# Attention probabilities go through an SBUF-to-SBUF transfer and are transposed as fp32r, with four lane steps from scores to transposes

## The chip, the cores and the metric

The kernel runs on one core of a Trainium2 chip. The metric is the device time of one execution in microseconds (us); less is better. TensorE is called PE below, VectorE DVE, ScalarE ACT, GpSimd POOL, and SyncE SP. SP issues nearly all transfers here, in one queue.

## What is computed

One layer of a bidirectional hybrid encoder is applied to two groups of tokens with the same weights: 1024 sample tokens (eight tiles of 128) and 256 prompt tokens (two tiles), width 2048. The input is normalised and projected, three groups of heads work on the projection, and their outputs are joined and projected back:

```
proj = rms_norm(x, norm_g) @ w_in
o_ssd = two chunked state-space scans (one per direction), gated and normalised
o_att = window attention of 8 heads: |t-s| <= 128, ALiBi, a sink logit per head
o_mem = attention of 4 heads to 256 memory rows:
    sm = einsum('bthd,bmhd->bhtm', mq, mk) * d ** -0.5
    pm = softmax(sm)
    o_mem = einsum('bhtm,bmhd->bthd', pm, mv) * silu(z_mem)
y = x + concat[o_ssd, o_att, o_mem] @ w_out
```

All data are fp32. The change lies in o_att and o_mem, between the softmax and the product with the values.

## The kernel before

**The main work** is the projections. Tokens are handled in two groups of five tiles. A weight block is walked in 16 steps of k (128 rows of the weights each). For every step, 256 KB of weights are loaded into a tile wraw (four buffers) and split by wsplit (L200) into a rounded high part wh (ACT, L202) and a rest wl (DVE, L203), three buffers each. Three products, high by high, low by high and high by low, then run as fp32r matmuls (L254 to L256 in block_tok, L289 to L291 in block_feat). In block_tok a step of k is 15 matmuls of 512 columns. In block_feat it is 12 of 320 columns.

**The side work** (attention, scan, preparation) is written as Python generators, put into two lanes by queue (L135). After each step of k, pump (L155) adds the block's rate (RATES, L32) to what each lane is owed and runs as many generator steps; a step ends at a yield. In block_feat the rates are halved. So a rate of 1.55 on lane 0 means that 1.55 yields of lane 0 pass in a step of k, and the number of yields between two parts of a generator sets how much main work is written between them. A scheduler then lists the instructions for every engine: an engine takes, in the order written, what its own model of times calls ready. The chip runs each engine's list strictly in order, and so does SP with its transfers: a transfer whose data are not there holds up all transfers behind it.

**Window attention**, attn(t) (L583), is on lane 0. For each of the ten token tiles it makes four rounds rr, each with one query head of either of two key groups kv. scores(rr) (L627) makes the scores on PE (psc, L635 and L636), adds the distance on DVE (L637), takes the exponential on ACT (L641) and scales by the sum on DVE (L645). The result stays in lg, two halves of 128 x 385 fp32 (256 of its columns are used for tiles at a sequence's end, 384 elsewhere). turn_(rr) (L649) transposes it on PE in blocks of 128 x 128 into ppt (L657) and copies that to pT on ACT (L658). values(half) (L662) multiplies with the values for two rounds.

**Memory attention**, mem_attn(t) (L697), is also on lane 0 and has two rounds of two heads: scores(hp) (L724) ends with L744 in a tile mpr of 128 x 512, turn_(hp) (L748) transposes it in four blocks into pmt (L752), and values(hp) (L761) follows.

The transposes of probabilities take fp32 data and an fp32 identity, ident. That is the fp32r tile identr under another type. Other transposes (pq L617, pk L501, pmq L713, pxs L843) take fp32r data and identr.

Working tiles of lane 0 share the tag wa, with five buffers (WA, L29): q, squares, split queries, gates and outputs. lg and mpr share the tag lg with two buffers.

Of the kernel before, what the change touches and what calls it, by code (L numbers as in the profile page):

```python
# [10 lines left out]
F32 = mybir.dt.float32  # L11
F32R = mybir.dt.float32r
# [7 lines left out]
P = 128  # L20
# [8 lines left out]
CH, WB, RB, WA, WBB = 4, 3, 4, 5, 4  # L29
RBB = 3  # L30

RATES = ({'kv': (2.0, 1.0), 'mq': (2.4, 1.6), 'z0': (2.2, 1.7), 'z1': (2.2, 1.7)},  # L32
         {'kv': (1.2, 1.5), 'x': (1.75, 1.85), 'q': (1.6, 2.5), 'za': (1.6, 2.5), 'z0': (1.55, 2.6),
          'z1': (1.55, 2.65), 'mq': (1.55, 2.8), 'zm': (1.55, 2.85), 'o': (1.95, 1.9)})
FAR = 1e30

UNITS = (0, 4, 1, 5, 2, 6, 7, 3, 8, 9)
# [6 lines left out]
def hymba_encoder_kernel(  # L44
# [7 lines left out]
    V, A, G, T, S = nc.vector, nc.scalar, nc.gpsimd, nc.tensor, nc.sync  # L52
# [33 lines left out]
    identr = const([P, P], "identr", F32R)  # L86
    ident = identr.bitcast(F32)
# [495 lines left out]
    def attn(t):  # L583
        lo, hi = (0, NS) if t < NS else (NS, NT)
        k0, k1 = max(lo, t - 1), min(hi, t + 2)
        na = k1 - k0
        nk = na * P
        d0 = (k0 - (t - 1)) * P
        s0 = k0 if t < 4 else k0 - 3
        grp, ti = divmod(t, 5)  # L590
        tc_ = slice(ti * P, (ti + 1) * P)
        q = w2("q")
        S.dma_start(q, q_d[t])
        yield
        sq = w2("sq")
        A.activation(sq, q, AF.Square)
        ss = sm.tile([P, 8], F32, tag="s8", name="qss", bufs=4)
        V.reduce_sum(out=ss, in_=hv(sq), axis=AX.X)
        r = sm.tile([P, 8], F32, tag="s8", name="qr", bufs=4)
        rsqrt(r, ss, 1.0 / 64, 8)  # L600
        G.tensor_tensor(out=r, in0=r, in1=steep, op=ALU.mult)
        for _ in range(3):
            yield
        q3 = hv(q)
        V.tensor_mul(q3, q3, hb(r, 8, 64))
        yield
        qT = []
        for b in range(2):
            qh = mp.tile([P, 4, 2, 64], F32R, tag="wa", name="qh", bufs=WA)
            qb = q3[:, 4 * b:4 * b + 4, :]  # L610
            A.activation(qh[:, :, 0, :], qb, AF.Copy)
            V.tensor_sub(qh[:, :, 1, :], qb, qh[:, :, 0, :].bitcast(F32))
            yield
            ps = psum("pq")
            qf = qh.rearrange("p a b d -> p (a b d)")
            for a in range(4):
                T.transpose(ps[:, a * P:(a + 1) * P].bitcast(F32R), qf[:, a * P:(a + 1) * P], identr)  # L617
            o = mp.tile([P, 512], F32R, tag="qT", name="qT", bufs=2)
            A.activation(o, ps, AF.Copy)
            qT.append(o)  # L620
        z = w2("za")
        S.dma_start(hv(z, 4), zT_d[0][grp][:, :, tc_])
        yield
        ns8 = nsink.rearrange("p (v r) -> p r v", v=2)
        state_ = {}

        def scores(rr):  # L627
            lg = mp.tile([P, 2, 385], F32, tag="lg", name="lg", bufs=2)
            G.tensor_copy(lg[:, :, nk:nk + 1], ns8[:, rr, :].unsqueeze(2))  # L629
            nm = sm.tile([P, 2], F32, tag="m2", name="nm", bufs=10)  # L630
            for kv in range(2):
                h = 4 * kv + rr
                ps = psum("psc")
                st = qT[kv][:, rr * P:(rr + 1) * P]
                T.matmul(ps[:, :nk], st, kT[:, kv, s0 * P:s0 * P + nk], start=True, stop=False)  # L635
                T.matmul(ps[:, :nk], st, kL[:, kv, s0 * P:s0 * P + nk], start=False, stop=True)  # L636
                V.tensor_tensor_reduce(out=lg[:, kv, :nk], in0=pdist[:, d0:d0 + nk], in1=ps[:, :nk], scale=2.0 ** -(h + 1),  # L637
                                       scalar=nsink[:, h:h + 1], op0=ALU.add, op1=ALU.min, accum_out=nm[:, kv:kv + 1])
            den = sm.tile([P, 2], F32, tag="m2", name="den", bufs=10)
            for kv in range(2):  # L640
                A.activation(lg[:, kv, :nk + 1], lg[:, kv, :nk + 1], AF.Exp, scale=-1.0, bias=nm[:, kv:kv + 1],  # L641
                             accum_out=den[:, kv:kv + 1])
            V.reciprocal(out=den, in_=den)
            for kv in range(2):
                V.tensor_scalar(out=lg[:, kv, :nk], in0=lg[:, kv, :nk], scalar1=den[:, kv:kv + 1], scalar2=0.5,  # L645
                                op0=ALU.mult, op1=ALU.mult)
            state_[rr] = lg

        def turn_(rr):  # L649
            lg = state_.pop(rr)  # L650
            if rr % 2 == 0:
                state_["pT"] = mp.tile([P, 2, 2, 384], F32, tag="pT", name="pT", bufs=1)
            pT = state_["pT"]
            for kv in range(2):
                pt = psum("ppt")
                for a in range(na):
                    T.transpose(pt[:, a * P:(a + 1) * P], lg[:, kv, a * P:(a + 1) * P], ident)  # L657
                A.activation(pT[:, kv, rr % 2, :nk], pt[:, :nk], AF.Copy)  # L658

        oT = w2("oT")  # L660

        def values(half):  # L662
            pT = state_.pop("pT")
            po = psum("po")
            for a in range(na):
                for kv in range(2):
                    T.matmul(hv(po[kv * 64:kv * 64 + 64, :2 * P], 2), v_all[:, s0 + a, kv * 64:kv * 64 + 64],  # L667
                             pT[:, kv, :, a * P:(a + 1) * P], start=(a == 0), stop=(a == na - 1))
            c = slice(half * 2 * P, (half + 1) * 2 * P)
            V.tensor_mul(oT[:, c], po[:, :2 * P], z[:, c])  # L670

        scores(0)
        yield
        scores(1)
        yield
        yield
        turn_(0)
        yield
        scores(2)
        yield  # L680
        turn_(1)
        yield
        scores(3)
        yield
        values(0)
        yield
        turn_(2)
        yield
        turn_(3)
        yield  # L690
        yield
        values(1)
        yield
        S.dma_start(oT_d[0][grp][:, :, tc_], hv(oT, 4))


    def mem_attn(t):  # L697
# [3 lines left out]
        q = qr.bitcast(F32)  # L701
# [20 lines left out]
        st_ = {}  # L722

        def scores(hp):  # L724
            ps = psum("pms")
            for j in range(2):
                h = 2 * hp + j
                c = slice(h * P, (h + 1) * P)
                o = ps[:, j * 256:(j + 1) * 256]
                T.matmul(o, qh[:, c], mkH[:, h, :], start=True, stop=False)  # L730
                T.matmul(o, qh[:, c], mkL[:, h, :], start=False, stop=False)
                T.matmul(o, ql[:, c], mkH[:, h, :], start=False, stop=True)
            m = sm.tile([P, 2], F32, tag="m2", name="mm", bufs=10)
            V.reduce_max(out=m, in_=hv(ps, 2), axis=AX.X)
            V.scalar_tensor_tensor(out=m, in0=m, scalar=-1.0, in1=r[:, 2 * hp:2 * hp + 2], op0=ALU.mult, op1=ALU.mult)
            pr = mp.tile([P, 512], F32, tag="lg", name="mpr", bufs=2)
            den = sm.tile([P, 2], F32, tag="m2", name="mden", bufs=10)
            for j in range(2):
                A.activation(pr[:, j * 256:(j + 1) * 256], ps[:, j * 256:(j + 1) * 256], AF.Exp,
                             scale=r[:, 2 * hp + j:2 * hp + j + 1], bias=m[:, j:j + 1], accum_out=den[:, j:j + 1])  # L740
            V.reciprocal(out=den, in_=den)
            for j in range(2):
                c = slice(j * 256, (j + 1) * 256)
                V.tensor_scalar(out=pr[:, c], in0=pr[:, c], scalar1=den[:, j:j + 1], scalar2=0.5,  # L744
                                op0=ALU.mult, op1=ALU.mult)
            st_[hp] = pr

        def turn_(hp):  # L748
            pr = st_[hp]
            pt = psum("pmt")  # L750
            for a in range(4):
                T.transpose(pt[:, a * P:(a + 1) * P], pr[:, a * P:(a + 1) * P], ident)  # L752
            if hp == 0:
                st_["pT"] = mp.tile([P, 2, 768], F32, tag="pT", name="mpT", bufs=1)
            pT = st_["pT"][:, hp, :512]
            A.activation(pT, pt, AF.Copy)
            st_[hp] = pT
# [13 lines left out]

        scores(0)
        yield
        scores(1)
        yield
        yield
        turn_(0)
        yield
        turn_(1)
        yield  # L780
        values(0)
        yield
        values(1)
        S.dma_start(oT_d[1][grp][:, :, tc_], hv(oT, 4))
# [713 lines left out]
    mp = beside.enter_context(tc.tile_pool(name="mp", bufs=2))  # L1498
# [178 lines left out]
```

## Time and profile before

| what | value |
|---|---|
| time, median of 3 runs | 1805.68 us (1805.18 to 1806.63) |
| the profiled execution's own time | 1804.94 us |
| its span, first to last instruction | 1803.2 us |
| PE busy | 1791.4 us (99%) |
| DVE, ACT, POOL busy | 1210.3, 902.3, 456.6 us |
| bytes moved | 290.58 MB, 161 GB/s on average |

In the profile, a group of instructions is told by line, engine, operation and the names of the tiles it writes and reads (out<-in). A busy time is the union of the instructions' durations. For matmuls those durations are modelled and overlap, so what one matmul costs the queue is read from the starts of neighbours or from the chain, not from its own duration. "Idle before" is the time in which the engine did nothing ahead of such an instruction, with what ended that. SPq is SP's own instruction stream.

### The profile page before, as it was taken

What the parts mean: (1) busy time and instruction counts of PE and PEld (TensorE: products, weight loads), DVE (VectorE), ACT (ScalarE), POOL (GpSimd) and SP (SyncE); (2) the same over time, 40 slices, a digit from 0 to 9 for tenths busy, and PEclk for the clock granted to TensorE, in tenths of its full rate; (3) what the DMA queues carried; (4) which work ended last, traced back from release to release, by engine and by line L of the source; (5) the groups of instructions that cost most, each with busy time, mean ns of one, the idle gap of its engine ahead of it and who ended that gap; (6) DMA issues with size and microseconds to landing.
All of it is one profiled execution on the core that took longest, in us unless ns stands there. A gap on an engine that the chain in (4) does not pass through costs nothing.

```text
span 1803.2 us, 30420 instructions
## 1 busy us (share of the span) xinstructions
PE 1791.4 (99%) x10546; PEld 1607.0 (89%) x10546; DVE 1210.3 (67%) x2303; ACT 902.3 (50%) x1999; POOL 456.6 (25%) x772
## 2 busy tenths in 40 slices
PE   9999999999999999999999999999999999999999
PEld 8789999999887799999989988887898888899999
DVE  5595788877657877675755766556775653867665
ACT  6554455444445756464435645544474533543332
POOL 0105888861110000000000001101100000058775
PEclk9999999999999999999999999999999999999999
DMA  8654454446544544344336355457785554644442
GB/s 299 190 178 122 137 151 152 126 134 217 168 134 152 177 133 139 121 132 133 118 95 192 113 164 173 128 181 233 230 269 162 180 189 142 215 154 147 141 144 79
DMA packets 198891, 290.58 MB, mean 161 GB/s; under 512 B 18960, under 2 KB 80464, under 8 KB 198736
## 3 DMA queue, kind: packets, MB, share of 16 engines
q1 hardware_dynamic: 198592, 288.57, 51.4%
q8 instruction: 83, 1.36, 0.3%
q14 instruction: 72, 0.59, 0.1%
q10 hardware_dynamic: 144, 0.06, 0.0%
HBM read 231.12 MB, written 57.44 MB: 160 GB/s over the span
## 4 chain that ended last, share of the span: by engine, by line
PE 87%; issue 5%; DMA 3%; DVE 2%; ACT 1%; POOL 1%; SPq 0%; ACTq 0%; DVEq 0%; POOLq 0%
PE acc L254 13%; PE acc L256 13%; PE acc L255 12%; PE acc L1194 6%; PE acc L1192 6%; PE acc L1193 6%; PE acc L289 5%; PE acc L290 4%; PE acc L291 4%; PE accm L1193 2%; PE accm L1192 2%; PE accm L1194 2%; PE py L924 2%; PE po L667 1%; PE ppt L657 1%
## 5 line engine op out<-in xcount | busy, mean ns | idle before, releaser
L203 DVE TENSOR_TENSOR wl<-wraw,wh 128x512 fp32r<-128x512 f32 (+1 forms) x480 | 340.5, 711 | 273.8 <-ACT wh L202 265.0
L254 PE MATMUL acc<-wh,xH 128*128 128x512 f32 (+1 forms) x1248 | 482.7, 387 | 0.2 <-ACT wh L202 0.2
L255 PE MATMUL acc<-wl,xH 128*128 128x512 f32 (+1 forms) x1248 | 472.2, 378 | 0.6 <-DVE wl L203 0.4
L256 PE MATMUL acc<-wh,xL 128*128 128x512 f32 (+1 forms) x1248 | 472.4, 379 | 0.0
L202 ACT ACTIVATE wh<-wraw 128x512 fp32r<-128x512 f32 (+1 forms) x480 | 293.4, 615 | 348.4 <-PE acc L256 189.5
L255 PEld LDWEIGHTS acc<-wl,xH 128*128 128x128 f32 x1248 | 234.9, 188 | 43.7 <-DVE wl L203 2.8
L254 PEld LDWEIGHTS acc<-wh,xH 128*128 128x128 f32 x1248 | 234.7, 188 | 43.6 <-issue 3.9
L256 PEld LDWEIGHTS acc<-wh,xL 128*128 128x128 f32 x1248 | 234.2, 188 | 43.4
L289 PE MATMUL acc<-xH,wh 128*128 128x320 f32 x640 | 203.9, 319 | 0.0
L290 PE MATMUL acc<-xL,wh 128*128 128x320 f32 x640 | 198.2, 310 | 0.0
L291 PE MATMUL acc<-xH,wl 128*128 128x320 f32 x640 | 198.0, 309 | 0.0
L202 ACT ACTIVATE sh<-ws 128x384 fp32r<-128x384 f32 x144 | 74.9, 525 | 180.9 <-POOL ws L1164 98.5
L203 DVE TENSOR_TENSOR sl<-ws,sh 128x384 fp32r<-128x384 f32 x144 | 100.1, 699 | 93.6 <-ACT sh L202 93.4
L1164 POOL TENSOR_TENSOR ws<-wraw 128x128 f32<-128x128 f32 x144 | 88.9, 617 | 202.5 <-DMA wraw<-in_w_in_pairs_dram 88.1
L629 POOL COPY lg<-nsink 128x2 f32<-128x2 f32 x40 | 16.5, 416 | 436.4 <-PE ppt L657 212.2
L289 PEld LDWEIGHTS acc<-xH,wh 128*128 128x128 f32 x640 | 120.3, 188 | 3.5 <-issue 2.7
L290 PEld LDWEIGHTS acc<-xL,wh 128*128 128x128 f32 x640 | 120.3, 188 | 2.3 <-issue 1.9
L291 PEld LDWEIGHTS acc<-xH,wl 128*128 128x128 f32 x640 | 120.2, 188 | 0.1
L1164 POOL TENSOR_TENSOR ws<-wraw,ws 128x128 f32<-128x128 f32 x144 | 94.6, 657 | 11.3
L358 DVE SCALAR_TENSOR_TENSOR c<-u,vec,c 128x638 f32<-128x638 f32 (+1 forms) x96 | 88.9, 931 | 11.2 <-ACT c L353 10.8
L1164 POOL TENSOR_TENSOR ws<-ws,wraw 128x128 f32<-128x128 f32 x144 | 93.3, 648 | 0.0
L1164 POOL TENSOR_TENSOR wraw<-wraw 128x128 f32<-128x128 f32 x144 | 89.1, 618 | 11.1
(426 smaller groups left out, 3601.3 us busy)
## 6 DMA issues: line engine op xcount, KB each, us to landing
wraw<-in_w_in_laid_dram SPq DMA_DIRECT2D x208, 256.0 KB, 2.8
wraw<-in_w_in_pairs_dram SPq DMA_DIRECT2D x80, 256.0 KB, 2.7
wraw<-in_w_out_laid_dram SPq DMA_DIRECT2D x64, 256.0 KB, 3.1
wraw<-in_w_out_pairs_dram SPq DMA_DIRECT2D x64, 256.0 KB, 2.8
rf<-ac SPq DMA_DIRECT2D x40, 256.0 KB, 3.6
rb<-ac SPq DMA_DIRECT2D x40, 256.0 KB, 4.0
wraw<-in_w_mem_laid_dram SPq DMA_DIRECT2D x32, 256.0 KB, 4.2
xst<-in_x_sample_dram SPq DMA_DIRECT2D x20, 256.0 KB, 4.9
```

The source lines that it names most:

```text
L202: a = A.activation(h, raw, AF.Copy)
L203: b = V.tensor_sub(l, raw, h.bitcast(F32))
L254: T.matmul(ps[t][:, :n], sh, h[:, :n], start=(k_ == 0), stop=False)
L255: T.matmul(ps[t][:, :n], sh, l[:, :n], start=False, stop=False)
L256: T.matmul(ps[t][:, :n], sl, h[:, :n], start=False, stop=(k_ == KT - 1))
L289: T.matmul(o, sh, cur["H", q][:, m, c], start=(k == 0), stop=False)
L290: T.matmul(o, sh, cur["L", q][:, m, c], start=False, stop=False)
L291: T.matmul(o, sl, cur["H", q][:, m, c], start=False, stop=(k == KT - 1))
L1164: G.tensor_tensor(out=o, in0=x, in1=y, op=op)
L1192: T.matmul(ps[p], h, xh, start=(k_ == 0), stop=False)
L1193: T.matmul(ps[p], h, xl, start=False, stop=False)
L1194: T.matmul(ps[p], l, xh, start=False, stop=(k_ == 7))
```

## The change

Three things are edited.

1. After the last scaling, the probabilities are copied by SP transfers into new fp32r tiles of the tag wa: two transfers per round in attn (lgR, one for each half) and one per round in mem_attn (mprR). The transpose then reads the copy, with identr, and writes its PSUM tile as fp32r. The transfer copies bits.
2. The yields are set so that four lane steps lie between scores and turn_ of every round. Before there were three or four in attn, and three in mem_attn. values(0) of mem_attn moves ahead of turn_(1). attn has one step more than before and mem_attn two.
3. The rates of lane 0 are raised by about 7%; those of lane 1 stay.

```diff
-RATES = ({'kv': (2.0, 1.0), 'mq': (2.4, 1.6), 'z0': (2.2, 1.7), 'z1': (2.2, 1.7)},
-         {'kv': (1.2, 1.5), 'x': (1.75, 1.85), 'q': (1.6, 2.5), 'za': (1.6, 2.5), 'z0': (1.55, 2.6),
-          'z1': (1.55, 2.65), 'mq': (1.55, 2.8), 'zm': (1.55, 2.85), 'o': (1.95, 1.9)})
+RATES = ({'kv': (2.14, 1.0), 'mq': (2.57, 1.6), 'z0': (2.35, 1.7), 'z1': (2.35, 1.7)},
+         {'kv': (1.28, 1.5), 'x': (1.87, 1.85), 'q': (1.71, 2.5), 'za': (1.71, 2.5), 'z0': (1.66, 2.6), 'z1': (1.66, 2.65), 'mq': (1.66, 2.8), 'zm': (1.66, 2.85), 'o': (2.09, 1.9)})
...
@@ attn
-            state_[rr] = lg
+            state_[rr] = [mp.tile([P, 384], F32R, tag="wa", name="lgR", bufs=WA) for _ in range(2)]
+            for kv in range(2):
+                S.dma_start(state_[rr][kv].bitcast(F32)[:, :nk], lg[:, kv, :nk])
...
-                    T.transpose(pt[:, a * P:(a + 1) * P], lg[:, kv, a * P:(a + 1) * P], ident)
+                    T.transpose(pt[:, a * P:(a + 1) * P].bitcast(F32R), lg[kv][:, a * P:(a + 1) * P], identr)
...
         scores(0)
         yield
+        yield
         scores(1)
         yield
         yield
         turn_(0)
-        yield
         scores(2)
         yield
+        yield
         turn_(1)
-        yield
         scores(3)
         yield
         values(0)
         yield
         turn_(2)
+        yield
         yield
         turn_(3)
         yield
@@ mem_attn
-            st_[hp] = pr
+            st_[hp] = mp.tile([P, 512], F32R, tag="wa", name="mprR", bufs=WA)
+            S.dma_start(st_[hp].bitcast(F32), pr)
...
-                T.transpose(pt[:, a * P:(a + 1) * P], pr[:, a * P:(a + 1) * P], ident)
+                T.transpose(pt[:, a * P:(a + 1) * P].bitcast(F32R), pr[:, a * P:(a + 1) * P], identr)
...
         scores(0)
         yield
+        yield
         scores(1)
         yield
         yield
         turn_(0)
         yield
+        values(0)
+        yield
         turn_(1)
         yield
-        values(0)
         yield
         values(1)
```

## The prediction

> **What bounds the kernel now.** I read the page first: busy times, the row of the granted clock, and the shares of the chain that ended last.
>
> ```profile
> span 1803.2 us, 30420 instructions
> PE 1791.4 (99%) x10546; PEld 1607.0 (89%) x10546; DVE 1210.3 (67%) x2303; ACT 902.3 (50%) x1999; POOL 456.6 (25%) x772
> PEclk9999999999999999999999999999999999999999
> PE 87%; issue 5%; DMA 3%; DVE 2%; ACT 1%; POOL 1%; SPq 0%; ACTq 0%; DVEq 0%; POOLq 0%
> ```
>
> PE is busy for 1791.4 of 1803.2 us, at full granted clock in every slice. So the end moves by what PE is spared, less the new time in which it stands still. Next comes the view of waits, for PE, ACT and SP:
>
> ```profile
> PE pmt L752 <- DVE mpr L744: 1.5, 2, 0.9
> PE ppt L657 <- DVE nm L637: 0.8, 2, 0.5
> ACT wh L202 <- PE acc L256: 189.5, 100, 4.5
> SPq L209 <- DVE wl L203: 331.7, 157, 7.6
> ```
>
> PE waits at the transposes in question for 1.5 + 0.8 = 2.3 us in all. The weight split on ACT waits 100 times for PE to give a buffer back, 189.5 us in all. SP's weight loads in their turn wait for the split. So weights stand ready ahead of PE, and the transfer queue has time in hand.
>
> **Part 1: what a transpose costs PE.** The count is in the groups, the price in the chain, where a run of equal instructions is one row (start, us, what).
>
> ```profile
> L657 PE MATMUL ppt<-identr,lg 128*128 128x128 f32 x208 | 31.1, 275 | 0.9 <-DVE nm L637 0.8
> L752 PE MATMUL pmt<-identr,mpr 128*128 128x128 f32 x80 | 12.0, 274 | 1.5 <-DVE mpr L744 1.5
> L843 PE MATMUL pxs<-identr,xc 128*128 128x128 f32 x80 | 9.5, 244 | 0.6 <-ACT pT L658 0.6
> L617 PE MATMUL pq<-identr,qh 128*128 128x128 f32 x80 | 8.9, 242 | 0.0
> ```
>
> ```profile
> 552.82 0.63 PE pq L617 x8
> 669.76 0.66 PE ppt L657 x6
> 1135.26 0.64 PE pxs L843 x8
> 1433.37 0.96 PE pmt L752 x8
> ```
>
> The fp32 transposes take 0.66 / 6 = 110 ns (ppt) and 0.96 / 8 = 120 ns (pmt). The transposes that already are fp32r, pq and pxs, take 0.63 / 8 and 0.64 / 8 = 80 ns. The gain is 208 x 30 ns = 6.2 us and 80 x 40 ns = 3.2 us, together **9.4 us**. The instruction counts on PE, DVE, ACT and POOL stay. Ends: with 110 ns for all it is 288 x 30 = 8.6 us. By the groups' busy unions a fp32 one is 31.1 / 208 = 150 ns, an fp32r one (9.5 + 8.9) / 160 = 115 ns, which gives 288 x 35 = 10.1 us.
>
> The Trainium skill speaks against this part: "TensorE: Matmul & The Clock Gate", Terms, has trn2's weight loads and matmuls gain a transpose mode that is four times faster for FP32. An fp32 transpose would then be as cheap as an fp32r one and the gain would be nil. The rows just shown agree with it by half: fp32 costs less than 1.5 times fp32r, but not the same.
>
> **Part 2: the copies and PE's wait for them.** There are 80 transfers of lgR (48 of 384 columns, 192 KB; 32 of 256, 128 KB) and 20 of mprR (256 KB), all on SP. No row shows a transfer inside SBUF, so the nearest ones, SBUF to DRAM, and one that reads DRAM as the far end (issuer, count, KB each, median us from issue to landing):
>
> ```profile
> mq<-qs SPq DMA_DIRECT2D x10, 256.0 KB, 2.6
> xbc_d<-u SPq DMA_DIRECT2D x12, 193.0 KB, 2.2
> yp<-ya SPq DMA_DIRECT2D x20, 256.0 KB, 3.6
> mq<-mq SPq DMA_DIRECT2D x10, 256.0 KB, 4.2
> ```
>
> I take 2.6 us, with 2.2 and 4.2 as ends: like mq<-qs, the copy leaves SBUF, and it is no bigger. The Trainium skill, "SBUF — State Buffer", The DMA setup-cost knee, fits 2 us plus the bytes at 436 GB/s, which would be an estimate of 2.45 us for 192 KB and 2.6 us for 256 KB. By that the sum below would come out about 0.5 us better; the trace's medians run from 2.2 to 4.2 us for such sizes.
>
> What the transfer is added to is the chain from the last scores matmul to the end of the scaling. One instance of each kind from the timeline (start, us), and one issue on SP:
>
> ```profile
> 606.75 0.34 PE L636 MATMUL psc<-kL,qT 128*128 128x384 f32 x1
> 609.74 0.74 DVE L645 TENSOR_SCALAR lg<-lg,den 128x384 f32<-128x384 f32 x2
> 609.87 0.33 SPq L835 DMA_DIRECT2D rf<-ac  x1
> ```
>
> ```profile
> 1466.73 0.28 PE L732 MATMUL pms<-mkH,mql 128*128 128x256 f32 x1
> 1470.48 0.61 DVE L744 TENSOR_SCALAR mpr<-mpr,mden 128x256 f32<-128x256 f32 x2
> ```
>
> In attn the scaling ends 609.74 + 0.74 - 606.75 = 3.73 us after the last scores matmul starts; in mem_attn 4.36 us. Today the transposes may start there. Now the second copy of a round is issued 0.33 us behind the first and lands 2.6 us later: 3.73 + 0.33 + 2.6 = 6.7 us. In mem_attn there is one copy: 4.36 + 2.6 = 7.0 us.
>
> Does PE have as much other work in between? One matmul of the main work is 0.23 us in the chain:
>
> ```profile
> 1430.42 0.23 PE acc L256
> ```
>
> A step of k is 15 of them, 3.45 us. Four lane steps at a rate of 1.66 are 4 / 1.66 x 3.45 = 8.3 us. Before, three steps at 1.55 were 6.7 us and four were 8.9 us. At 2.35 (group 0, z blocks) four are only 5.9 us. The program as built shows it turn by turn, since the order on PE is fixed: I priced the PE instructions between the last scores matmul of each round and its first transpose by their intervals in this trace (0.23 us for 512 columns, 0.15 for 320, and so on). Before, the 60 gaps have a median of 8.4 us and a least of 4.0. Now the median is 9.4 us and the least 4.6 (the first tile, in z0). Six of 60 fall short of 6.7 or 7.0 us, by **3.5 us** in all. At a landing of 2.2 us three fall short, by 1.8 us; at 3.6 us 15, by 13.0 us; at 4.2 us 22, by 24.3 us.
>
> The same reckoning for the kernel before, with 3.73 and 4.36 us, gives 1.2 us where the trace has 2.3: chains scatter around one instance, and turns close to the edge pay for it, 1.1 us for the eight within 1 us of it. Now 15 are that close, so I choose twice that, 2.2 us, on top of 3.5: 5.7 us. The old 2.3 us go, so PE stands still **3.4 us** longer.
>
> **What the copies hold up.** SP is in order. A copy at its head waits for DVE; behind it stand weight loads, the ac rows (rf, rb), gates and queries. I cost this at nothing: SP is already stopped at its head 157 times by L203 alone, up to 7.6 us, and PE does not feel it because splits wait for PE and not for weights (the ACT row above). If that cover were gone, each of 60 rounds could hold weights back by up to its chain of 4 us, but the cover is seven buffers deep (four wraw, three wh), some 24 us of matmuls. Some copies also wait for PE to free a wa buffer; as built, such a freeing stands at least 5.4 us of PE work ahead of the transpose in question, more than issue and landing, so it costs nothing unless the landing is at its far end.
>
> **Moved steps and rates.** attn has 13 side steps for 12 from its first scores on, mem_attn nine for seven, and lane 0 runs 7% faster; the amounts cancel nearly, and PE's lists are the same up to the first memory preparation, L444. What is reshuffled behind it can shift single stalls by a few tenths either way; all PE idle time is 1803.2 - 1791.4 = 11.8 us, so I put plus or minus 2 us in the range for it and nothing in the sum.
>
> **Sum.** Against the profiled execution's 1804.94 us (1803.2 of span and 1.7 around it): -9.4 + 3.4 = -6.0 us, 1798.9 us. That execution lies 0.74 us below the median of the runs, 1805.68 us. From the median the forecast is **1799.7 us**.
>
> **The rivals.**
>
> *The copies are hidden (R1).* They land after 2.2 us as the 193 KB rows do. Shortfall 1.8 us and 1.1 for scatter are 2.9 us, 0.6 more than today: -9.4 + 0.6 = -8.8 us, **1796.9 us**. For it: SBUF may answer sooner than DRAM. Against: the 256 KB weight loads share the queue.
>
> *The copies land late and PE waits for them (R2, the other side).* The place is turn_, whose transposes stand in PE's list ahead of main work that could run. At 3.6 us, the row of yp<-ya, PE is short by 13.0 us, 10.7 more than today: +1.3 us, **1807.0 us**, no change that can be told. At 4.2 us, the row of mq<-mq, it is short by 24.3: -9.4 + 22.0 = +12.6 us, **1818.3 us**. It turns into a loss beyond 0.2% when the shortfall passes 9.4 + 2.3 + 3.6 = 15.3 us, at a landing near 3.7 us. For it: 256 KB writes have medians up to 3.6 us, since they come in bursts with other loads, as the copies will. Against: one PE wait gives the next round's copy time, so shortfalls don't all add.
>
> *fp32r saves nothing here (R3).* Then only the waits are left: +3.4 us, **1809.1 us**. Against it stand 110 and 120 beside 80 ns; for it, that a row of pq may be cheap for another reason than its type, such as its neighbours.
>
> **How the numbers follow.** The forecast (1798 to 1803) has 0.46, R1 0.17, R2 0.27, half of it at landings short of 3.7 us and half beyond, R3 0.06, and 0.04 is for lists reshuffled to a loss. About 0.2%, 3.6 us, is what a measurement of this kernel can tell from no change: faster means below 1802.1, slower above 1809.3 us. Faster takes R1 and nine tenths of the forecast: 0.58. Slower takes half of R2, half of R3, and the 0.04: 0.2, of which I leave 0.03 to the middle because waits help each other: 0.17. The same is 0.25. The range goes from the full gain of 10.1 us with no new wait, 1795.6, to R2 at its 3.6 us row, 1807.0, with a little of the reshuffling: 1795.5 to 1808.
>
> **What would show it.** Right: ppt and pmt at about 80 ns apiece in the chain; rows of PE waiting for lgR and mprR of some 6 us together, mostly in z0 (the first tile) and mem_attn; landings of lgR near 2.6 us; no wait of PE for wh or wl that was not there. R1 would show less than 3 us of such waits, R2 landings over 3.6 us and a dozen or more turns waiting, R3 x6 rows of 0.66 us for ppt still. The prediction is wrong in its frame if PE comes to wait for weights, or if ACT or DVE turns out later in front of the transposes than 3.73 and 4.36 us, so that the scaling itself is late.

## The result and the profile after

| what | before | after |
|---|---|---|
| median of 20 runs each, on one chip | 1806.35 us (1804.36 to 1811.92) | 1803.8 us (1800.68 to 1805.69) |
| the profiled execution's own time | 1804.94 us | 1804.15 us |

The ratio after to before is 0.9985, with a 95% interval of 0.9978 to 0.9992: 2.55 us faster. That is inside the range and has the sign of the forecast. It is less than half of the 6.0 us that were forecast, and by the prediction's bound of 0.2% it counts as the same, to which the prediction gave a chance of 0.25. Two more comparisons of the same kernel, below, gave 0.9986 and 0.9993.

The page of the kernel after, its span, busy times and the chain's shares:

```profile
span 1802.4 us, 30786 instructions
PE 1789.5 (99%) x10546; PEld 1600.9 (89%) x10546; DVE 1211.0 (67%) x2303; ACT 901.0 (50%) x1999; POOL 457.4 (25%) x772
PE 88%; issue 4%; DMA 4%; DVE 2%; ACT 1%; POOL 1%; SPq 0%; ACTq 0%; DVEq 0%; POOLq 0%
```

PE is busy for 1.9 us less than before, not 9.4 us less. It is still the bound, and DMA's share of the chain went from 3% to 4%. Next the groups by form (busy, mean ns, idle before) and, from the view of DMA issues, the landings (count, KB each, median us):

```profile
L658 PE MATMUL ppt<-identr,lgR 128*128 128x128 f32 x208 | 26.0, 250 | 2.4 <-DMA lgR<-lg 2.4
L755 PE MATMUL pmt<-identr,mprR 128*128 128x128 f32 x80 | 9.7, 244 | 0.6 <-DVE c L357 0.6
```

```profile
lgR<-lg SPq DMA_DIRECT2D x48, 192.0 KB, 2.2
mprR<-mpr SPq DMA_DIRECT2D x20, 256.0 KB, 2.4
lgR<-lg SPq DMA_DIRECT2D x32, 128.0 KB, 3.5
```

The transposes' unions fell from 31.1 to 26.0 and from 12.0 to 9.7 us, 7.4 us together. But a union is a modelled figure, and the next section shows that it is not what the queue was spared. The larger copies land in 2.2 to 2.4 us. The smallest are the slowest: they fall where the queue is fullest. In the trace the 16 DMA engines are busy for 0.81 of the time around them in the median, against 0.54 around the 192 KB ones, and the quickest of them landed in 1.9 us. The view of PE's waits (us in all, times, longest):

```profile
PE ppt L658 <- DMA lgR<-lg: 2.4, 2, 1.4
PE psc L634 <- ACT pT L659: 1.5, 2, 0.9
PE acc L254 <- DVE wl L202: 0.8, 4, 0.2
PE pmt L755 <- DVE c L357: 0.6, 1, 0.6
```

Three turns wait, for 2.4 + 0.6 = 3.0 us. They stand at 756, 1265 and 1345 us, not at the first tile. (For the one at 755.59 us the profile names DVE's c as the last to come, but its copy had landed only at 755.46, so it is counted here.) A row that was not looked for is the second: the scores matmul (L634) waits 1.5 us for pT, which is not the copy's landing at all.

### The profile page after: what moved, and what is told of

It is laid out like the page before. It is cut to its first block, busy times and chain, and to the rows that moved or that the text cites. A ratio compares the mean times of both kernels' runs of the same rounds, so it can differ in the third digit from the quotient of the medians.

```text
span 1802.4 us, 30786 instructions
## 1 busy us (share of the span) xinstructions
PE 1789.5 (99%) x10546; PEld 1600.9 (89%) x10546; DVE 1211.0 (67%) x2303; ACT 901.0 (50%) x1999; POOL 457.4 (25%) x772
## 4 chain that ended last, share of the span: by engine, by line
PE 88%; issue 4%; DMA 4%; DVE 2%; ACT 1%; POOL 1%; SPq 0%; ACTq 0%; DVEq 0%; POOLq 0%
PE acc L253 13%; PE acc L255 12%; PE acc L254 12%; PE acc L1199 6%; PE acc L1197 6%; PE acc L1198 6%; PE acc L288 5%; PE acc L289 5%; PE acc L290 5%; PE accm L1198 2%; PE accm L1197 2%; PE accm L1199 2%; PE py L929 2%; PE po L668 1%; PE pmo L770 1%
## 5 line engine op out<-in xcount | busy, mean ns | idle before, releaser
L628 POOL COPY lg<-nsink 128x2 f32<-128x2 f32 x40 | 11.5, 288 | 412.1 <-DMA lgR<-lg 214.8
```

## The price of a transpose, read again

The traces alone answer the first question, what a transpose costs PE. What one run of transposes costs is the time from its start until PE is back at its usual pace. In the timeline of the kernel before, a run of six fp32 ones, in a stretch of matmuls that start every 0.147 us (start, duration):

```profile
718.72 0.82 PE L657 MATMUL ppt<-identr,lg 128*128 128x128 f32 x6
719.29 0.39 PE L289 MATMUL acc<-xH,wh 128*128 128x320 f32 x1
719.52 0.31 PE L290 MATMUL acc<-xL,wh 128*128 128x320 f32 x1
```

The same in the timeline of the kernel after, with six fp32r ones:

```profile
657.81 0.63 PE L658 MATMUL ppt<-identr,lgR 128*128 128x128 f32 x6
658.27 0.38 PE L288 MATMUL acc<-xH,wh 128*128 128x320 f32 x1
658.49 0.30 PE L289 MATMUL acc<-xL,wh 128*128 128x320 f32 x1
```

From the run's start to the second matmul behind it, less one interval of 0.147 us, it is 719.52 - 718.72 - 0.15 = 0.65 us before and 658.49 - 657.81 - 0.15 = 0.53 us after. The first matmul behind the run is late in both types: its neighbour follows after 0.22 to 0.23 us and not 0.147, some 75 ns that belong to the run. Medians over all runs of a length, reckoned so:

| transposes in a run | fp32, us | fp32r, us |
|---|---|---|
| 4 | 0.439 | 0.368 |
| 6 | 0.657 | 0.539 |
| 8 | 0.874 | 0.708 |
| 12 (the doubling experiments below) | 1.313 | 1.053 |

These are 109 ns for each fp32 one, and 85 ns for each fp32r one plus 27 ns for a run. The saving is 18 ns apiece in runs of four, 20 in runs of six, 21 in runs of eight: 288 times 18 to 20 ns, some **5 to 6 us**, not 9.4.

Where did 80 ns come from? From the chain view, whose rows of one kind I had set against rows of another. These are the rows behind those two in the kernel before, the first matmul behind pq x8 and the one behind pmt x8:

```profile
553.45 0.30 PE acc L254
...
1434.33 0.23 PE acc L254
```

Behind the fp32r run the next matmul has 0.30 us, 0.07 more than usual; behind the fp32 run it has its usual 0.23, and the 0.07 are inside the run's own row. With it, pq costs (0.63 + 0.07) / 8 = 88 ns against 110 to 120. The 120 ns of pmt came from that single row of eight; its other rows without a wait in the chain, in runs of four, are 0.44 to 0.46 us, 110 to 115 ns apiece. All of this was in the trace before the change.

## The experiments

For the rest three questions were open. Is the price above what the time shows? Do the yields and rates matter? And what do the copies cost: only what PE waits at the turns for their landing, or also what they hold up in SP's queue for others (theory Q)? Ratios are to the kernel before on the same chip, with the 95% interval.

**Copies with fp32 kept.** The tiles of the copies are fp32 and the transposes take ident; yields and rates are the change's.

```diff
-            state_[rr] = [mp.tile([P, 384], F32R, tag="wa", name="lgR", bufs=WA) for _ in range(2)]
+            state_[rr] = [mp.tile([P, 384], F32, tag="wa", name="lgR", bufs=WA) for _ in range(2)]
...
-                    T.transpose(pt[:, a * P:(a + 1) * P].bitcast(F32R), lg[kv][:, a * P:(a + 1) * P], identr)
+                    T.transpose(pt[:, a * P:(a + 1) * P], lg[kv][:, a * P:(a + 1) * P], ident)
```

> The changed kernel with its copies, yields and rates, but the copies are fp32 tiles and the transposes stay fp32. Theory A (a run of n transposes costs PE about 110 ns x n in fp32 and 78 ns x n + 60 ns in fp32r, the 60 ns falling on the matmul behind the run, so the type saves 18 to 20 ns each, 5.3 us in all): 5.3 us slower than the changed kernel, which is 2.5 us faster than before, so 2.8 us slower than before (ratio about 1.0015). Theory B (my prediction's price, 30 to 40 ns each, 9.4 us, with waits for copies having eaten the rest): 9.4 us slower than the changed kernel, 6.9 us slower than before (1.004).

Measured: 1809.77 us against 1804.85, 1.0023 (1.0013 to 1.0034), 4.2 us slower than before by the ratio, 4.9 by the medians. That lies between the 2.8 us of theory A and the 6.9 of theory B. The copies and the steps by themselves lose.

**Steps and rates alone.** Only the yields and rates of the change; no copy, fp32 transposes of lg and mpr.

```diff
-            state_[rr] = [mp.tile([P, 384], F32R, tag="wa", name="lgR", bufs=WA) for _ in range(2)]
-            for kv in range(2):
-                S.dma_start(state_[rr][kv].bitcast(F32)[:, :nk], lg[:, kv, :nk])
+            state_[rr] = [lg[:, kv] for kv in range(2)]
```

> Only the yields and rates of the change; no copies, transposes fp32 out of lg and mpr. Theory A and B: PE waits less at the transposes (2.3 us before), so 0 to 2 us faster than before (0.999 to 1.000). Theory C (the new placing of the side work itself costs time, whatever is transposed): 2 us or more slower than before (1.001 or more).

Measured: 1805.33 us, 1.0002 (0.9993 to 1.0011): nothing. Its page:

```profile
PE 1793.4 (100%) x10546; PEld 1605.7 (89%) x10546; DVE 1210.7 (67%) x2303; ACT 900.8 (50%) x1999; POOL 461.0 (26%) x772
```

PE's listed waits fall from 7.6 us in all before to 4.5, and its busy time rises by 2.0 us (1791.4 to 1793.4). What follows: steps and rates are neutral in time, and what the run above has beyond this one is the copies': 1809.77 - 1805.33 = 4.4 us.

**No copies: the scaling writes fp32r tiles.** DVE's last scaling writes lgR and mprR itself, which rounds the probabilities to fp32r; nothing is transferred. Once with the yields and rates of before, once with those of the change.

```diff
-                S.dma_start(state_[rr][kv].bitcast(F32)[:, :nk], lg[:, kv, :nk])
+                V.tensor_scalar(out=state_[rr][kv][:, :nk], in0=lg[:, kv, :nk], ...)
...
-            S.dma_start(st_[hp].bitcast(F32), pr)
+                V.tensor_scalar(out=st_[hp][:, c], in0=pr[:, c], ...)
```

> The last scaling on DVE writes the fp32r tiles itself, which rounds the probabilities; no copies; yields and rates of before. The only thing that changes for PE is the type of the 288 transposes. Theory A: 5.3 us faster than before (0.9971). Theory B: 9.4 us faster than before (0.9948).

> As the one before, with the yields and rates of the change: the changed kernel without its copies, with rounded probabilities. Theory A: the changed kernel loses 2 to 3 us to PE waiting for copies, so this is 5 to 6 us faster than before (0.997). Theory B: the copies cost the changed kernel 7 us, so this is 9 to 11 us faster than before (0.9945). Theory C (placing costs): about as fast as the changed kernel, 2.5 us faster than before (0.9986).

Measured: 1798.61 us, 0.9964 (0.9952 to 0.9977), with the old steps; 1797.9 us, 0.9960 (0.9947 to 0.9972), with the new. The transposes' type is worth 6.5 us against before and 7.4 us against the kernel with the steps alone; the scheduler's lists move with it, so this is the type with what the lists make of it. It is a little more than the 5 to 6 us of the timelines. The intervals against before are 4.2 to 8.7 us and 5.1 to 9.6 us, so it is the timelines and not these runs that exclude 9.4. Both beat the two kernels of this case. The page of the second:

```profile
PE 1788.3 (100%) x10546; PEld 1601.2 (89%) x10546; DVE 1212.5 (67%) x2303; ACT 900.2 (50%) x1999; POOL 457.8 (25%) x772
```

This also tells why PE's busy time fell by 1.9 us only: from before it goes up by 2.0 with the steps (1793.4), down by 5.1 with the type (1788.3) and up by 1.2 with the copies (1789.5).

**Each transpose made twice.** The prices by the clock of the runs: each of the 288 transposes is issued twice in a row, in the kernel before (fp32) and in the changed kernel (fp32r).

```diff
-                    T.transpose(...)
+                    for _ in range(2):
+                        T.transpose(...)
```

> The kernel before with each of the 288 transposes of probabilities made twice in a row into the same place (the second repeats the first, so the result stays). Every run doubles in length and none is added. Theory A (fp32: 110 ns for each, nothing for the run): 288 x 110 ns = 31.7 us slower than before (1.0176). A rival with a flat 90 ns and a fixed cost for each run in fp32: 26 us (1.0144).

> The changed kernel with each of the 288 transposes made twice in a row. Theory A (fp32r: 78 ns for each, and a fixed 60 ns for the run that is not paid again): 288 x 78 ns = 22.5 us slower than the changed kernel, about 20 us slower than before (1.011). Rival (what the matmul behind a run pays belongs to each transpose, 92 ns flat): 26.5 us slower than the changed kernel, 24 us slower than before (1.0133).

Measured: 1834.94 us, 1.0168 (1.0154 to 1.0182), for fp32: 30.4 us more than before on this chip (1804.57), 30.4 / 288 = 105 ns for one more. And 1827.08 us, 1.0126 (1.0112 to 1.0140), for fp32r: 25.1 us more than the changed kernel (1801.99, next run), 87 ns for one more. That lies between the 78 and the 92 ns that the two readings of the price gave. The difference of the types is 18 ns, 5.3 us for 288; each interval is some 2.5 us to either side. A run of twelve in the timeline of the fp32r kernel:

```profile
728.82 1.13 PE L659 MATMUL ppt<-identr,lgR 128*128 128x128 f32 x12
729.78 0.38 PE L288 MATMUL acc<-xH,wh 128*128 128x320 f32 x1
730.00 0.31 PE L289 MATMUL acc<-xL,wh 128*128 128x320 f32 x1
```

That is 730.00 - 728.82 - 0.15 = 1.03 us, twelve times 86 ns. The prices of the table hold by two ways of measuring.

**The changed kernel again, and with a fifth step.** The first is the same kernel once more; the second puts one more yield between scores and turn_ of each round and raises lane 0's rates by 5.5%, so that copies have more time to land.

```diff
-          'z0': (1.66, 2.6), ... 'o': (2.09, 1.9)
+          'z0': (1.75, 2.6), ... 'o': (2.20, 1.9)
...
         scores(1)
         yield
         yield
+        yield
         turn_(0)
```

> The changed kernel itself, unaltered, beside the next three on one chip. Both theories: about 2.5 us faster than before (0.9985), as measured.

> The changed kernel with five lane steps from scores to transposes for four, rates of lane 0 5.5% higher. Theory A (copies cost about 4 us because PE waits for them to land at a few tight turns): the waits for lgR go from 2.4 us to under 1 us, and the time falls 1 to 3 us below the changed kernel. Rival (the copies cost by something else, such as their use of the transfer queue, or the placing takes back what the waits give): within 1 us of the changed kernel or slower.

Measured: 1801.99 us, 0.9986 (0.9977 to 0.9995), and 1801.33 us, 0.9982 (0.9974 to 0.9991): the same. PE's waits in the changed kernel run again:

```profile
PE psc L634 <- ACT pT L659: 1.6, 1, 1.6
...
PE ppt L658 <- DMA lgR<-lg: 0.8, 1, 0.8
PE pmt L755 <- DMA mprR<-mpr: 0.7, 2, 0.4
```

and with five steps:

```profile
PE psc L634 <- ACT pT L659: 2.3, 1, 2.3
```

With five steps no turn waits for a landing any more, and the time stays: the wait for pT is 2.3 us and not 1.6, and the table further down has this kernel gain 1.8 us on the changed one before 1307 us and lose 1.6 us after 1369 us, where the changed one loses nothing. Had the landings been all, some 1.5 us would have gone for good, though 0.7 us (1801.99 to 1801.33) is within what the intervals leave open.

**Copies that PE does not wait for.** The kernel without copies and with the new steps (e4), and in it the 100 transfers of the change, issued at the same places, the other way round: from the fp32r tiles back into lg and mpr, which nobody reads after that. The transposes do not wait for them; only the next writer of those buffers does, as in the changed kernel.

```diff
                 V.tensor_scalar(out=state_[rr][kv][:, :nk], in0=lg[:, kv, :nk], ...)
+                S.dma_start(lg[:, kv, :nk], state_[rr][kv].bitcast(F32)[:, :nk])
...
+            S.dma_start(pr, st_[hp].bitcast(F32))
```

> The changed kernel's yields and rates; DVE scales straight into the fp32r tiles (rounding the probabilities) and PE transposes those without waiting for a transfer. The 100 copies are still issued, from the fp32r tiles back into lg and mpr, which nobody reads after that. Theory W (the copies cost 4 to 5 us because PE waits for their landing): as fast as the version without copies, 0.996 of before. Theory Q (they cost it by their place in SP's queue, their bytes, or the tiles that they hold): as slow as the changed kernel, 0.9986 of before.

**Copies in window attention only.** mem_attn as in the kernel without copies, attn as in the change.

> The changed kernel with copies in attn only; mem_attn scales straight into the fp32r tile, which rounds its probabilities. If the cost of the copies goes with the waits of the trace (lgR 0.8 to 2.4 us, mprR 0.6 to 0.7): most of it stays, 0.998 of before. If it goes with the number of copies (80 of 100) likewise; if memory attention is where it falls: 0.9965.

Beside these two ran the kernel without copies (e4) and the changed kernel once more:

> The version without copies at the change's yields and rates once more, beside the two before: 0.996 of before, 4 to 5 us faster than the changed kernel.

> The changed kernel once more, on the same chip as the three before: 0.9986 of before.

Measured, against 1803.52 us before: e7 1801.45 us, 0.9991 (0.9982 to 1.0000); e8 1801.76 us, 0.9987 (0.9978 to 0.9996); e4 again 1797.85 us, 0.9967 (0.9955 to 0.9980); the changed kernel 1801.73 us, 0.9993 (0.9984 to 1.0002). On one chip, copies that PE does not wait for cost 1801.45 - 1797.85 = 3.6 us, as much as the 3.9 us of copies that PE does wait for. Theory Q holds: the landings at the turns are not needed for the loss. Which part of it, the place in SP's queue, the bytes or the tiles that are held, these times do not tell. Leaving out the 20 copies of mem_attn changes nothing that can be told.

Where e7 loses shows when the matmuls of the projections' products are counted in PE's order and the start of the same one is compared with that in e4 again. Positive is later, in us; the columns are stretches of e4 again, cut at such matmuls:

| kernel | 481 to 1307 us | 1307 to 1369 us | 1369 to 1516 us |
|---|---|---|---|
| e7, copies not waited for | -0.2 | +3.3 | 0 |
| changed, the three executions | +2.0, +2.0, +2.5 | +3.1, +2.2, +2.7 | 0, 0, -0.1 |
| e8, copies in attn only | +1.2 | +3.2 | 0 |
| e4, its first execution | +0.2 | +0.6 | 0 |
| e6, five steps | +0.2 | +2.6 | +1.6 |
| e3, no copies, old steps | +1.4 | -1.0 | +1.7 |
| before | +4.6 | +0.4 | +2.1 |
| e2, steps alone, fp32 | +4.8 | +2.0 | +0.4 |
| e1, copies with fp32 | +8.5 | +2.9 | +0.9 |

Before 481 us, where PE's lists are all the same, these executions differ by about -1 to +3 us, so a whole trace says little about 2 us and these stretches, each from its own start, say more. After 1516 us nothing differs by more than 0.6 us. In e7 3.3 of the 3.5 us by which its span is longer lie in 62 us, around the hand-over to the output projection: a group's outputs are written to DRAM (oT<-so), read back (chd<-oT), and split by ACT into xH (L195). Every kernel with copies loses 2.2 to 3.3 us in that stretch, e4 0 and 0.6. But e2 loses 2.0 there without any copy, so the copies are not the only thing that can push it; and e1, which is e2 with copies, loses only 0.9 more there and 3.7 more before 1307 us. Since e7's PE is level with that of e4 again until then, their rows can be set side by side. (Transfers that are added also make the scheduler list the engines anew. In this stage the order on ACT is the same in both up to the copy of pT, the order on SP is not.) SP's timeline in e7 (start, us):

```profile
1315.11 0.55 SPq L994 DMA_DIRECT2D oT<-so  x1
...
1316.79 0.55 SPq L994 DMA_DIRECT2D oT<-so  x1
1317.44 1.46 SPq L648 DMA_DIRECT2D lg<-lgR  x2
1320.55 0.33 SPq L183 DMA_DIRECT2D chd<-oT  x1
...
1322.41 1.11 SPq L648 DMA_DIRECT2D lg<-lgR  x2
1323.58 1.41 SPq L183 DMA_DIRECT2D chd<-oT  x2
```

and in e4 again:

```profile
1315.04 0.52 SPq L991 DMA_DIRECT2D oT<-so  x1
...
1317.10 0.52 SPq L991 DMA_DIRECT2D oT<-so  x1
1319.60 0.33 SPq L183 DMA_DIRECT2D chd<-oT  x1
...
1320.49 1.33 SPq L183 DMA_DIRECT2D chd<-oT  x3
```

The first read back goes out as soon as the last write but one has landed, 5.4 us after its issue in e7 and 4.5 us in e4 again; so it comes at 1320.55 and not at 1319.60. The second comes at 1321.87 for 1320.49, with two transfers of rb<-ac between the two reads for one, and lands after 6.6 us and not 5.4. The third and fourth have two more copies ahead of them in e7 and come at 1323.58 for some 1321. On ACT, in order as well, the splits of the first two reads then wait; those of the third and fourth do not. In the ACT timeline of e7 (in brackets: idle before, and for what):

```profile
1323.67 0.83 ACT L195 ACTIVATE xH<-chd,vec 128x640 fp32r<-128x640 f32 x1 [0.64 <-DMA chd<-oT]
...
1328.44 0.83 ACT L195 ACTIVATE xH<-chd,vec 128x640 fp32r<-128x640 f32 x1 [1.28 <-DMA chd<-oT]
...
1333.45 0.67 ACT L659 ACTIVATE pT<-ppt 128x256 f32<-128x256 f32 x2
```

and of e4 again, where neither split waits for chd:

```profile
1323.24 0.82 ACT L195 ACTIVATE xH<-chd,vec 128x640 fp32r<-128x640 f32 x1
...
1326.57 0.82 ACT L195 ACTIVATE xH<-chd,vec 128x640 fp32r<-128x640 f32 x1
...
1331.67 0.65 ACT L657 ACTIVATE pT<-ppt 128x256 f32<-128x256 f32 x2
```

The copies of pT stand behind the splits on ACT and come 1.8 us later. PE's waits of e7 have this row:

```profile
PE psc L634 <- ACT pT L659: 2.0, 1, 2.0
```

That is 2.0 of the 3.3 us. The rest follows behind the wait: PE's granted clock falls to half. The view of windows of e7 (window, us, busy us and instructions of PE, PEld, DVE, ACT and POOL, granted clock, DMA share, GB/s):

```profile
1332.00:1334.80 2.80, 0.91 (x7) 0.80 (x7) 2.80 (x7) 2.80 (x9) 0.00 (x0) 1.00 0.99 316
1334.90:1338.20 3.30, 3.30 (x14) 1.93 (x14) 2.85 (x9) 2.10 (x9) 0.00 (x0) 0.50 0.84 274
1338.30:1341.70 3.40, 3.40 (x20) 2.77 (x19) 2.17 (x4) 3.05 (x8) 0.00 (x0) 1.00 0.93 334
```

and of e4 again:

```profile
1334.90:1338.20 3.30, 3.30 (x20) 2.68 (x18) 3.29 (x9) 3.30 (x9) 0.00 (x0) 1.00 0.82 250
```

PE counts as busy in both, but 14 matmuls stand in this window of e7 and 20 in that of e4 again. The trace has the clock at 0.50 for 3.41 us, from 1334.86 on, which is 1.7 us of work lost; 2.0 and 1.7 are 3.7 us, of which 0.4 are won back by 1369 us. The page does not show it, since 3.4 us are little in a slice of 45 us. The changed kernel run again, e8 and e6 have the same 3.41 us at half clock behind waits of 1.6, 1.7 and 2.3 us. The first and third executions of the changed kernel (0.9 and 1.2 us) do not, and lose 1.4 and 0.9 us to a landing at 1345 us in the same stretch instead; e1 does not either, behind 1.6 us. What brings the clock down is thus not settled here. In the runs, a mean granted clock of 0.999 and not 1.000 goes with it in every execution that was traced: 1.7 of 1800 us. It is listed in 7 of 11 runs of e7, 5 of 11 of e8, 6 of 11 of e6 and 14 of 42 of the changed kernel, in 2 of 11 of e1 and 1 of 11 of e2, in 5 of 69 of before and in none of 15 of the kernels without copies (e3 and e4).

The late pT itself is not the copies' alone. The first execution of e4 has this row, at the same place:

```profile
PE psc L634 <- ACT pT L657: 1.1, 1, 1.1
```

There the second read lands after 6.8 us, its split waits 1.1 us, and PE loses 1.1 us, half of which it wins back; the clock stays.

In the changed kernel run again, the chain (start, us, what) runs through the round trip, write and read:

```profile
1316.49 5.25 DMA oT<-so
1321.81 4.26 DMA chd<-oT
...
1334.60 0.28 ACT pT L659
1334.92 0.39 PE psc L634
```

PE's wait for pT there is 0.9 to 2.3 us in all traces of kernels with copies; without copies it is 1.1 and 0 us in e4, 0.3 in e2, and not listed in e3 and before. From the issue of the last write but one to the landing of the first read it is 8.3 to 10.5 us in the traces with copies and 8.0 to 9.0 us without, so the two overlap, and only against e4 (8.0 and 8.1) are all of them longer. The chain is thus: a longer round trip, ACT's split at the head of its list, pT late, PE's next scores late, and at times half the clock for 3.4 us behind that. e7 shows that copies cost without being waited for, and its trace shows the place. That the round trip is the link is read from the rows; no run moved the round trip alone or kept the lists while it added transfers, and copies with the yields of before were not run either.

## Why the prediction was right in sign and short in size

**Part 1, 9.4 us: the step that failed.** It took 80 ns for an fp32r transpose from chain rows in which the cost to the next matmul is left out, beside 110 and 120 ns in which it is contained. The like-for-like price is 85 ns and 27 ns a run against 109: 5 to 6 us by timelines, 5.3 by the doubled transposes, 6.5 to 7.2 by the kernels without copies. The sign that was to show it right did come. The chain now has for a run of six, and the matmul behind it,

```profile
657.97 0.47 PE ppt L658 x6
658.44 0.22 PE acc L288
```

78 ns apiece; 18 of the 21 rows of six are 0.46 or 0.47 us, and the matmul behind has 0.07 us more than usual. But this sign was read in the same rows as the price and left out the same cost, so it could not tell 9.4 us from 5 to 6. The low end, 8.6 us, had the same fault, and the high end, 10.1 us, came from busy unions, which are modelled. R3 (fp32r saves nothing) is refuted, by the 6.5 us. The rule weighed there, the Trainium skill, "TensorE: Matmul & The Clock Gate", Terms (a transpose mode four times faster for FP32), cannot be the whole of it either: with it the two types should cost alike, and they stand at 109 to 85 ns.

**Part 2, landings: right for 68 of the 100 copies.** 2.6 us were taken, 2.2 and 2.4 came for lgR of 192 KB and mprR. The Trainium skill, "SBUF — State Buffer", The DMA setup-cost knee, gave 2.45 and 2.6 us as estimates, and these rows agree within 0.3 us. The 128 KB copies took 3.5 us, more than the larger ones, since the queue is busy there.

**Part 2, the waits for them: too large, and elsewhere.** 5.7 us at turns in z0 and mem_attn were forecast. The three executions of the changed kernel have 3.0, 1.5 and 2.2 us: 0.6 to 0.7 of each in mem_attn, the rest not in z0 but at 1265 and 1345 us, where the 128 KB copies are slow. The shortfall of 3.5 us and the doubled scatter of 2.2 did not come in that size. These waits are near the mark of R1 (less than 3 us), though its time, 1796.9 us, rests on the price of Part 1 and did not come. With five steps these waits go, without a gain that can be told.

**What the copies hold up, costed at nothing: wrong.** The weights had the cover that was named: PE's rows for wh and wl stay under 1 us each. But I asked only who waits for weights behind a copy. SP also carries the round trip of the outputs through DRAM, whose reader on ACT has pT behind it. e7 prices what the copies cost beside their landings at 3.6 us. In its trace 3.3 us lie at this round trip: 2.0 of waiting, and the rest behind it at half the granted clock, which the prediction did not reckon with.

**Steps and rates, nothing in the sum: right.** 1.0002.

**The sum.** Forecast were -9.4 and, for the copies, +3.4. Measured are about -6.5 for the type and +4 for the copies, -2.5 us. That the copies' total came out near the forecast is luck: two errors cancel, less at the turns, more at the hand-over. It is luck too that the time lies inside the range, whose upper part was there for late landings (R2). The miss is the price of Part 1.

**Open.** e7's median is 0.3 us from the changed kernel's, though its trace is about 2 us ahead of it up to 1307 us; the intervals of some 1.6 us to either side cannot tell whether that is so in the runs. By what the copies lengthen the round trip, and what halves the clock behind some waits and not others, is not shown. And the type is worth 5.3 us by doubling and up to 7.2 us by the kernels without copies, a difference within their intervals.

## What to carry to other kernels

Take the price of a run of short instructions from its start to where the neighbours are back at their pace, for both kinds alike; a chain row may or may not contain what the run costs the next instruction. When a transfer is added to an in-order queue, list every reader downstream of that queue, down to what stands behind that reader on its own engine; cover for the heaviest stream (here weights) says nothing of the others. Look at the granted clock in windows of a few us around a wait of the bounding engine: here some waits of 2 us were followed by 3.4 us at half clock, which cost nearly as much again and which neither the page nor the view of waits shows. Here the conversion was better left to an engine that writes the tile anyway: 1797.9 us with DVE writing fp32r, at rounded probabilities, against 1802 to 1804 with exact copies.

## What the runs showed of the hardware

A 128 x 128 transpose at full granted clock costs PE 109 ns in fp32 and 85 ns in fp32r, and a matmul behind a run of them starts its neighbour some 75 ns late in both types. Transfers inside SBUF landed in 2.2 us for 192 KB and 2.4 us for 256 KB; SBUF to DRAM took 2.6 us for 193 KB and 2.7 us for 256 KB in the same trace (xbc_d<-u, mq<-qs), and 2.2 and 2.6 us in the kernel before. In four traces the granted clock fell to half for 3.41 us behind a wait of PE of 1.6 to 2.3 us, and in one it did not behind 1.6 us. A hundred of these transfers, which PE did not wait for, cost 3.6 us of 1800.
